# Seven block products for gate and up, and a separate down stage fed through DRAM, in a two-layer hybrid encoder step

## The chip, the core and the metric

The kernel runs on one NeuronCore of a Trainium2 chip. The metric is the device time of one execution in microseconds; lower is better. The core has five engines that run side by side, each through its own list of instructions in a fixed order: TensorE (PE in the tables; its weight loads are PEld), VectorE (DVE), ScalarE (ACT), GpSimd (POOL) and SyncE (SP), which here only starts transfers. An engine that waits for something holds up all that stands behind it in its list.

## What is computed

Two layers of a streaming encoder act on nine tiles of 128 rows (eight of a prompt, and one, number 4 in the kernel's order, with eight decoding streams of 16 rows), each 1024 wide. Each layer has three mixers, an output projection with a layer norm, and a feed-forward block. Only the last is changed:

```python
def conv_ffn(x, conv_prev, w_gate, w_up, conv_w, conv_b, w_down):
    hg = x @ w_gate
    hu = x @ w_up
    ext = jnp.concatenate([conv_prev.astype(hg.dtype), hg], axis=1)
    conv = conv_b + sum(conv_w[j] * ext[:, j:j + t] for j in range(CONV_W))
    return (jax.nn.gelu(conv) * hu) @ w_down, ext[:, t:]

def finish(...):
    x = layer_norm(ALPHA * x + mix @ w_out, ln1_g, ln1_b)
    f, conv_state = conv_ffn(x, conv_prev, w_gate, w_up, conv_w, conv_b, w_down)
    x = layer_norm(ALPHA * x + f, ln2_g, ln2_b)
```

`w_gate` and `w_up` are 1024 x 2816, `w_down` is 2816 x 1024. The 2816 columns are handled as 22 blocks f of 128.

## The kernel before

Every large product is done on float32 numbers that are split in two float32r parts, a high part h (a cast, on ScalarE) and a low part l (the difference, on VectorE or GpSimd). `mm3` (L171) makes one product of three matmuls: h with h, h with l, l with h. Weights come from DRAM as slabs: `load_slab` (L103) fetches a raw half, casts it, subtracts, and puts the parts in one of two buffers; `next_slab` (L141) hands them out in the order of the list `plan`.

After the mixers each layer has these stages. **w_out**: `w_out` adds the output projection to the residual tiles `x1s[j]`, tiles 0 to 4 (`G1`) among the last of the attention, tiles 5 to 8 (`G2`) after it; `norm1` normalises them, and `transpose_into` turns them (TensorE, L201) into `xts[j]`, split by `put_hl` (L191, L192). **Gate and up**: for each f, `gate_up` makes the gate product over three groups of columns (320, 320 and 512 of the 1152 rows), `conv_in` and `conv` apply the convolution and the GELU, then come three up products, `gated` multiplies and splits the result into `ah` and `al`, which stay in SBUF. **Down**: after block 0, and then after every three blocks (`FG`), `down` makes 18 products (nine tiles, two halves of the output) and VectorE adds each to `x1s[j]` (L1322). In the last of these eight passes `norm2` (L224 to L230) normalises each tile when it is done; in layer 0 the tiles are turned for the next layer (`ready`, three tiles behind), in layer 1 they are the output.

Inside one engine the order is set by the program's order and by a scheduler that moves an instruction ahead of others where it is ready earlier. What stands in the list runs in that order.

## Time and profile before

| | us |
|---|---|
| median of three runs (3004.11 to 3006.88) | 3004.44 |
| the profiled execution, its own time | 3001.13 |
| its span, first to last instruction | 2999.4 |
| TensorE busy in the span | 2902.6 (97%) |
| VectorE busy | 1773.2 (59%) |
| ScalarE busy | 1250.6 (42%) |
| GpSimd busy | 612.4 (20%) |

All sums are made against the profiled execution. It lies 3.3 us under the median. A busy TensorE is not yet one at its best: matmuls overlap, so how long one takes is read from the distance between two starts, not from its own duration. Where TensorE is busy without a gap, only fewer or shorter matmuls shorten the stage; where it has gaps, the wait that ends last decides.

### The profile page before, as it was taken

What the parts mean: (1) busy time and instruction counts of PE and PEld (TensorE: products, weight loads), DVE (VectorE), ACT (ScalarE), POOL (GpSimd) and SP (SyncE); (2) the same over time, 40 slices, a digit from 0 to 9 for tenths busy, and PEclk for the clock granted to TensorE, in tenths of its full rate; (3) what the DMA queues carried; (4) which work ended last, traced back from release to release, by engine and by line L of the source; (5) the groups of instructions that cost most, each with busy time, mean ns of one, the idle gap of its engine ahead of it and who ended that gap; (6) DMA issues with size and microseconds to landing.
All of it is one profiled execution on the core that took longest, in us unless ns stands there. A gap on an engine that the chain in (4) does not pass through costs nothing.

```text
span 2999.4 us, 47327 instructions
## 1 busy us (share of the span) xinstructions
PE 2902.6 (97%) x18356; PEld 2642.0 (88%) x18356; DVE 1773.2 (59%) x4110; ACT 1250.6 (42%) x2685; POOL 612.4 (20%) x737
## 2 busy tenths in 40 slices
PE   9999999999999999999999999999999999999997
PEld 8898898998898898898788988989988988988986
DVE  6899777764334334334779996777643333333337
ACT  6588566543222222222356884666331222222212
POOL 3344433420000000000343445334100000000003
PEclk9999999999999999999999999999999999999998
DMA  4211123121111111111222111131211111111112
GB/s 137 62 47 53 41 60 114 45 85 43 50 36 43 50 36 43 50 36 39 100 64 82 44 44 45 47 113 38 92 53 39 36 53 39 36 53 39 36 50 80
DMA packets 79071, 168.92 MB, mean 56 GB/s; under 512 B 18278, under 2 KB 38654, under 8 KB 78846
## 3 DMA queue, kind: packets, MB, share of 16 engines
q1 hardware_dynamic: 71022, 159.99, 16.5%
q10 hardware_dynamic: 7824, 5.90, 0.6%
q8 instruction: 145, 2.38, 0.3%
q14 instruction: 80, 0.66, 0.1%
HBM read 146.60 MB, written 19.25 MB: 55 GB/s over the span
## 4 chain that ended last, share of the span: by engine, by line
PE 84%; DVE 9%; issue 2%; POOL 2%; ACT 2%; DMA 1%; SPq 0%; ACTq 0%; DVEq 0%; POOLq 0%
PE pg L173 12%; PE pg L174 12%; PE pg L175 12%; PE pdn L174 6%; PE pdn L173 6%; PE pdn L175 6%; PE pwo L173 2%; PE pwo L175 2%; PE pwo L174 2%; PE pvg L173 2%; PE pvg L174 2%; PE pvg L175 2%; PE tp L980 1%; DVE spare L555 1%; PE lgi L411 1%
## 5 line engine op out<-in xcount | busy, mean ns | idle before, releaser
L173 PE MATMUL pg<-xg,slab_h 128*128 128x320 f32 (+1 forms) x2112 | 709.0, 336 | 1.1 <-ACT xg L191 1.1
L174 PE MATMUL pg<-xg,slab_h 128*128 128x320 f32 (+1 forms) x2112 | 709.8, 336 | 0.0
L175 PE MATMUL pg<-xg,slab_l 128*128 128x320 f32 (+1 forms) x2112 | 709.1, 336 | 0.0
L173 PEld LDWEIGHTS pg<-xg,slab_h 128*128 128x128 f32 x2112 | 396.4, 188 | 30.2 <-ACT xg L191 1.6
L175 PEld LDWEIGHTS pg<-xg,slab_l 128*128 128x128 f32 x2112 | 396.5, 188 | 28.2
L174 PEld LDWEIGHTS pg<-xg,slab_h 128*128 128x128 f32 x2112 | 396.4, 188 | 27.7
L113 ACT CAST slab_h<-raw 128x1024 fp32r<-128x1024 f32 (+3 forms) x154 | 140.5, 959 | 628.9 <-PE pdn L175 426.1
L1322 DVE SCALAR_TENSOR_TENSOR x<-x,pdn 128x512 f32<-128x512 f32 x288 | 194.5, 684 | 251.0 <-PE pdn L175 249.1
L173 PE MATMUL pdn<-slab_h,ah 128*128 128x512 f32 x792 | 312.5, 395 | 0.0
L174 PE MATMUL pdn<-slab_l,ah 128*128 128x512 f32 x792 | 312.2, 395 | 0.0
L175 PE MATMUL pdn<-slab_h,al 128*128 128x512 f32 x792 | 312.1, 394 | 0.0
L561 ACT ACTIVATE spare<-sc,cand 128x384 bf16<-128x384 f32 (+4 forms) x262 | 244.5, 933 | 67.6 <-DVE cand L587 27.9
L1256 DVE SCALAR_TENSOR_TENSOR ct<-hx,cwt,ct 128x1024 f32<-128x1024 f32 x88 | 113.1, 1285 | 229.9 <-ACT ct L1252 228.3
L1259 POOL COPY tails<-hx 128x16 f32<-128x16 f32 x44 | 9.4, 214 | 1121.5 <-ACT hx L1249 1121.5
L1268 DVE TENSOR_TENSOR ct<-ct,pg 128x320 f32<-128x320 f32 x132 | 72.8, 554 | 233.6 <-PE pg L175 174.2
L121 POOL TENSOR_TENSOR slab_l<-raw,slab_h 128x512 fp32r<-128x512 f32 (+1 forms) x140 | 188.5, 1374 | 102.2 <-ACT slab_h L120 99.9
L175 PEld LDWEIGHTS pdn<-slab_h,al 128*128 128x128 f32 x792 | 149.2, 188 | 34.9
L174 PEld LDWEIGHTS pdn<-slab_l,ah 128*128 128x128 f32 x792 | 149.2, 188 | 34.5
L173 PEld LDWEIGHTS pdn<-slab_h,ah 128*128 128x128 f32 x792 | 149.2, 188 | 34.5
L114 DVE TENSOR_TENSOR slab_l<-raw,slab_h 128x1024 fp32r<-128x1024 f32 (+3 forms) x154 | 166.3, 1112 | 15.7 <-ACT slab_h L113 15.6
L173 PE MATMUL pwo<-slab_h,xg 128*128 128x256 f32 x576 | 165.3, 287 | 0.3
L175 PE MATMUL pwo<-slab_h,xg 128*128 128x256 f32 x576 | 162.9, 283 | 0.6 <-DVE xg L997 0.6
(323 smaller groups left out, 6713.2 us busy)
## 6 DMA issues: line engine op xcount, KB each, us to landing
raw<-w_gu SPq DMA_DIRECT2D x88, 512.0 KB, 4.2
raw<-w_d SPq DMA_DIRECT2D x56, 384.0 KB, 3.6
raw<-w_s SPq DMA_DIRECT2D x40, 512.0 KB, 4.2
raw<-w_o SPq DMA_DIRECT2D x32, 512.0 KB, 4.5
ml<-mixd SPq DMA_DIRECT2D x18, 320.0 KB, 3.0
x<-x SPq DMA_DIRECT2D x9, 512.0 KB, 6.2
xd<-x SPq DMA_DIRECT2D x9, 512.0 KB, 3.0
x<-xd SPq DMA_DIRECT2D x9, 512.0 KB, 7.5
```

The source lines that it names most:

```text
L113: nc.scalar.copy(h[:, s], raw)
L114: eng.tensor_tensor(l[:, s], raw, h[:, s].bitcast(F32), ALU.subtract)
L121: eng.tensor_tensor(l[:, t], raw[:, r], h[:, t].bitcast(F32), ALU.subtract)
L173: nc.tensor.matmul(out, lh, rh, start=first, stop=False)
L174: nc.tensor.matmul(out, lh, rl, start=False, stop=False)
L175: nc.tensor.matmul(out, ll, rh, start=False, stop=last)
L411: nc.tensor.matmul(lg[:, :wh], qTs[j][:, h, :], kflat[:, s], start=True, stop=True)
L555: nc.vector.tensor_scalar(junkv[:, :w], sc[i], cand[q][:, c:c + 1].bitcast(F32), float(kof(i) - w), op0=ALU.is_lt, op1=ALU.add, accum_out= ...
L561: nc.scalar.activation(junka[:, :w], sc[i], AF.Sign, bias=cand[q][:, c:c + 1].bitcast(F32), scale=-1.0, accum_out=dst)
L1256: nc.vector.scalar_tensor_tensor(cpr, hp[s_], cwt[:, f, s_:s_ + 1], cpr, op0=ALU.mult, op1=ALU.add)
L1268: nc.vector.tensor_tensor(ct[:, cs], ct[:, cs], pg[1, c][:, :w], ALU.mult)
L1322: nc.vector.scalar_tensor_tensor(x1s[j][:, cs], x1s[j][:, cs], ALPHA if g == 0 else 1.0, po, op0=ALU.mult, op1=ALU.add)
```

## The change

For each f the matrix of weights is seen as two by two blocks: gate and up, times the two halves of the 1024 inputs (A11, A12 for gate, A21, A22 for up). The inputs are seen as two by two blocks too: the halves of the 1024 inputs, times two sets of rows (prompt tiles 0 to 3 with half of the decoding rows, 5 to 8 with the other half). The four results, which took eight block products, are made of seven, by Winograd's form of Strassen's method:

- Four combinations of the weights, S1 to S4, are made for each f by GpSimd (`wnext`: four instructions of 128x512), then split like any weight.
- Four combinations of the inputs, T1 to T4, are made once for each layer, in `pair` for tiles 5 to 8 and in `pair_dec` for the decoding rows, on GpSimd, VectorE and ScalarE. All operands stay in SBUF: `ar` holds B11, B21, T3 and T4, `ara` B22, `arb` T1, `art` T2.
- A product (`product`) has 24 matmuls for each of two groups of 288 columns over half of the inputs: 12 of each. Its result lies in two PSUM banks. Four such pairs of banks are there.
- VectorE adds the seven results up (`add`, `gate_in`), then come convolution, GELU and multiplication as before.
- The gated rows of each f are written to DRAM (`ad`) in float32, not split. The down stage comes after all 22 blocks: six passes (`FD`: 2, then five times 4 blocks), for which `load_a` and `load_w` fetch and split rows and weights again. The sums are held in new tiles `acc[j]`: ScalarE copies the first pass, VectorE adds the others, and the residual, which was saved to DRAM (`x1d`), is added in passes 2 and 3.
- Weights everywhere go through one tile `ring`, whose parts are laid out by hand. The tiles of the next layer (`xts`) share `ar` with the gated rows of the last pass, so that tiles 4 to 8 are turned only after its last matmul; before, this was so for fewer of them.

```diff
-FG = [(0, 1)] + [(f, 3) for f in range(1, 22, 3)]
+FD = [(0, 2), (2, 4), (6, 4), (10, 4), (14, 4), (18, 4)]
...
+        def pair(j, where):
+
+            va, vb = turned_x(x1s[j], where)
+            at = cols_of(j - 5)
+            t1, t2, t3 = (temp().rearrange("p (k t) -> p k t", k=4) for _ in range(3))
+            nc.scalar.copy(t3, va)
+            sub2(at, t1, "B11", t3, (G, G))
+            put(at, "B22", vb, V)
+            V.tensor_tensor(t2, vb, t1, ALU.subtract)
+            V.tensor_tensor(t3, vb, t3, ALU.subtract)
+            put(at, "T1", t1, V)
+            put(at, "T2", t2, V)
+            rsub2(at, t2, "B21", t2, (G, G))
+            put(at, "T3", t3, V)
+            put(at, "T4", t2, V)
...
         def norm1(j):
             if j in G2:
                 norm_rows(x1s[j], xp1)
             affine_rows(x1s[j], gt, bt, NORM1[j])
+            nc.scalar.dma_start(x1d[j], x1s[j])
...
+            if n == "S2":
+                G.tensor_tensor(tail[:, 0:512], a21, a22, ALU.add)
+                G.tensor_tensor(a21, a11, a21, ALU.subtract)
+                G.tensor_tensor(a11, tail[:, 0:512], a11, ALU.subtract)
+            if n == "S4":
+                G.tensor_tensor(a12, a12, a11, ALU.subtract)
+            h, l = wslot((4 + i) % 8)
+            nc.scalar.copy(h, src)
+            V.tensor_tensor(l, src, h.bitcast(F32), ALU.subtract)
...
+        def product(n, f, x):
+
+            h, l = aw.pop((n, f))
+            xo, b = opx[x], banks("pg")
+            for c in range(2):
+                cs = slice(288 * c, 288 * c + 288)
+                for k in range(4):
+                    mm3(b[:, c, :288], h[:, k, :], l[:, k, :], xo[:, 0, k, cs], xo[:, 1, k, cs], k == 0, k == 3)
...
+        first = [product("A11", 0, "B11")]
+        pair(5, where())
+        pair(6, where())
+        first.append(product("A12", 0, "B21"))
+        pair(7, where())
+        pair(8, where())
+        pair_dec()
...
-            for k in range(KC):
-                    mm3(b[:, :w], hv[:, a, k, :], lv[:, a, k, :], xg[:, 0, k, x0:x0 + w], xg[:, 1, k, x0:x0 + w],
-                        k == 0, k == KC - 1)
...
+        for f in range(NF):
+            b1, b2 = first if f == 0 else (product("A11", f, "B11"), product("A12", f, "B21"))
...
+            nc.scalar.copy(s1, b1[:, :, :288])
+            gate_in(f, 0, s1, b2)
+            add(s1, s1, product("S2", f, "T2"))
...
+            add(s2, s1, product("S1", f, "T1"))
+            gate_in(f, 1, s2, product("S4", f, "B22"))
+            conv(f)
+            b7 = product("S3", f, "T3")
+            add(s2, s2, b7)
+            add(s3, s1, b7)
+            gated(f, 1, s2)
+            add(s3, s3, product("A22", f, "T4"))
+            gated(f, 0, s3)
+            nc.scalar.dma_start(ad[f], ct[f % 2])
...
+                if g == 0:
+                    nc.scalar.copy(acc[j][:, cs], po)
+                else:
+                    V.tensor_tensor(acc[j][:, cs], acc[j][:, cs], po, ALU.add)
+                if u % 4 == 0 and nxt:
+                    f = nxt.pop(0)
+                    load_a(f)
+                    load_w(g + 1, f)
```

Three places of the order matter. The first is TensorE's list where gate and up begin, before: `pg` is a product of gate and up, `trx` the turning of a tile, and tiles 5 to 8 (`x1_5` to `x1_8`) are turned after four products of block 0.

```order
L175 MATMUL pg_8996<-xg1_79,slab_l_8736 128x320
L201 MATMUL trx_9021<-identr_72,x1_5_8297 128x128 x4
L201 MATMUL trx_9028<-identr_72,x1_5_8297 128x128 x4
L201 MATMUL trx_9035<-identr_72,x1_6_8299 128x128 x4
L201 MATMUL trx_9042<-identr_72,x1_6_8299 128x128 x4
L201 MATMUL trx_9049<-identr_72,x1_7_8301 128x128 x4
L201 MATMUL trx_9056<-identr_72,x1_7_8301 128x128 x4
L201 MATMUL trx_9063<-identr_72,x1_8_8303 128x128 x4
L201 MATMUL trx_9070<-identr_72,x1_8_8303 128x128 x4
L173 MATMUL pg_9084<-xg2_80,slab_h_8735 128x512
```

The same place of TensorE's list in the changed kernel, where the second product (`pg_8984`, A12 with B21) ends: `art` is T2 and `arb` is T1.

```order
L178 MATMUL pg_8984<-ar_75,ring_76 128x288
L1238 MATMUL trx_9009<-identr_66,x1_7_8280 128x128 x8
L1238 MATMUL trx_9035<-identr_66,x1_8_8282 128x128 x8
L176 MATMUL pg_9113<-art_8891,ring_76 128x288
L176 MATMUL pg_9141<-arb_8269,ring_76 128x288
```

Two products stand ahead of the last turning instead of four, and the matmul behind it reads T2, which needs all four tiles and the decoding rows. GpSimd's list at that place, in the changed kernel, for tiles 7 and 8 and the beginning of the decoding rows (`x12d`); `tail` is the temporary for T1, `temp0` that for T2 and T4, `temp1` that for T3:

```order
L1261 TENSOR_TENSOR tail_77<-temp1_8274,ar_75 128x512
L1267 TENSOR_TENSOR temp0_8273<-temp0_8273,ar_75 128x512
L1262 TENSOR_TENSOR tail_77<-tail_77,ar_75 128x512
L1266 TENSOR_TENSOR temp0_8273<-ar_75,temp0_8273 128x512
L1261 TENSOR_TENSOR tail_77<-temp1_8274,ar_75 128x512
L1267 TENSOR_TENSOR temp0_8273<-temp0_8273,ar_75 128x512
L1262 TENSOR_TENSOR tail_77<-tail_77,ar_75 128x512
L1261 TENSOR_TENSOR tail_77<-x12d_8275,ar_75 128x256
L1266 TENSOR_TENSOR temp0_8273<-ar_75,temp0_8273 128x512
```

GpSimd had only a few copies of at most 16 columns at this place before; now four instructions of 128x512 stand there for each of four tiles and twelve of half that size for the decoding rows, and every tile uses the same three temporaries. VectorE's list there, in the changed kernel, for one tile (6; the first row and the last two are its neighbours'):

```order
L1229 TENSOR_TENSOR ar_75<-temp0_8273,ar_75 128x4x128
L1279 TENSOR_TENSOR temp0_8273<-trx_8958,tail_77 128x512
L1280 TENSOR_TENSOR temp1_8274<-trx_8958,temp1_8274 128x512
L1229 TENSOR_TENSOR arb_8269<-tail_77,arb_8269 128x4x128
L1229 TENSOR_TENSOR art_8891<-temp0_8273,art_8891 128x4x128
L1229 TENSOR_TENSOR ar_75<-temp1_8274,ar_75 128x4x128
L1229 TENSOR_TENSOR ara_8268<-trx_9009,ara_8268 128x4x128
L1229 TENSOR_TENSOR ar_75<-temp0_8273,ar_75 128x4x128
```

T2's temporary is written only after the low part of the former tile's T4 (the first row), and GpSimd's second pair of instructions waits for the low part of T2 (the fifth).

## Rows read from the trace of the kernel before

**Rows 1.** Page, part 1: busy time, share of span, instructions of each engine
```profile
PE 2902.6 (97%) x18356; PEld 2642.0 (88%) x18356; DVE 1773.2 (59%) x4110; ACT 1250.6 (42%) x2685; POOL 612.4 (20%) x737
```

**Rows 2.** Windows: from:to, length, busy by engine (instructions), granted clock, DMA share, GB/s
```profile
654.60:1484.30 829.70, 828.12 (x4401) 733.98 (x4400) 344.78 (x495) 211.04 (x341) 29.67 (x99) 1.00 0.14 45
...
2148.20:2980.50 832.30, 831.61 (x4403) 736.39 (x4401) 349.11 (x499) 209.03 (x336) 32.95 (x101) 1.00 0.14 44
2980.50:2999.40 18.90, 0.00 (x0) 0.00 (x0) 15.08 (x18) 2.48 (x2) 9.86 (x6) 0.59 0.35 139
```

**Rows 3.** Timeline, TensorE, gate and up: start, duration (us), engine, line, operation
```profile
999.74 0.31 PE L174 MATMUL pg<-xg,slab_h 128*128 128x320 f32 x1
...
1003.85 0.31 PE L175 MATMUL pg<-xg,slab_l 128*128 128x320 f32 x1
...
1005.38 0.39 PE L173 MATMUL pg<-xg,slab_h 128*128 128x512 f32 x1
...
1009.23 0.39 PE L175 MATMUL pg<-xg,slab_l 128*128 128x512 f32 x1
```

**Rows 4.** Timeline, TensorE, w_out: products of 256 columns
```profile
634.97 0.28 PE L173 MATMUL pwo<-slab_h,xg 128*128 128x256 f32 x1
...
639.88 0.28 PE L175 MATMUL pwo<-slab_h,xg 128*128 128x256 f32 x1
```

**Rows 5.** Timeline, TensorE, where tiles 5 to 8 are turned in layer 0
```profile
668.85 3.66 PE L201 MATMUL trx<-identr,x 128*128 128x128 f32 x32
673.06 0.88 PE L173 MATMUL pg<-xg,slab_h 128*128 128x512 f32 x3 [0.56 <-ACT xg L191]
```

**Rows 6.** Timeline, VectorE, end of norm1 of tiles 7 and 8 in layer 0
```profile
664.72 2.35 DVE L230 TENSOR_TENSOR x<-x,ct 128x1024 f32<-128x1024 f32 x2
```

**Rows 7.** Groups by form, GpSimd: count, busy us, mean ns, idle before
```profile
L121 POOL TENSOR_TENSOR slab_l<-raw,slab_h 128x512 fp32r<-128x512 f32 x136 | 182.8, 1371 | 102.0 <-ACT slab_h L120 99.8 <-PE lg L949 2.0
...
L366 POOL TENSOR_TENSOR vbuf<-vbuf,both 128x256 f32<-128x256 f32 x2 | 1.5, 732 | 0.0
```

**Rows 8.** Groups by form, VectorE
```profile
L1256 DVE SCALAR_TENSOR_TENSOR ct<-hx,cwt,ct 128x1024 f32<-128x1024 f32 x88 | 113.1, 1285 | 229.9 <-ACT ct L1252 228.3
...
L1257 DVE SCALAR_TENSOR_TENSOR ct<-hx,cwt,ct 128x128 f32<-128x128 f32 x88 | 31.0, 352 | 192.0 <-ACT ct L1252 190.5
L1268 DVE TENSOR_TENSOR ct<-ct,pg 128x512 f32<-128x512 f32 x44 | 30.2, 687 | 166.1 <-PE pg L175 166.1
L1270 DVE TENSOR_TENSOR al<-ct,ah 128x512 fp32r<-128x512 f32 x44 | 30.1, 685 | 0.0
```

**Rows 9.** Groups by form, ScalarE
```profile
L191 ACT CAST xg<-trx 128x512 fp32r<-128x512 f32 x72 | 39.3, 605 | 27.2 <-PE trx L201 27.2
```

**Rows 10.** Timeline, VectorE, end of layer 1
```profile
2976.27 1.21 DVE L229 TENSOR_TENSOR x<-x,hx 128x1024 f32<-128x1024 f32 x1
...
2979.45 1.66 DVE L229 TENSOR_TENSOR x<-x,hx 128x1024 f32<-128x1024 f32 x1
...
2985.13 0.68 DVE L1322 SCALAR_TENSOR_TENSOR x<-x,pdn 128x512 f32<-128x512 f32 x1
```

**Rows 11.** Timeline, GpSimd, the same place
```profile
2977.62 2.41 POOL L230 TENSOR_TENSOR x<-x,ct 128x1024 f32<-128x1024 f32 x1 [1.24 <-DVE bnsc L224]
```

**Rows 12.** Windows of 4 us where layer 1 begins, columns as in rows 2
```profile
1492.00:1496.00 4.00, 0.00 (x0) 0.00 (x0) 4.00 (x7) 0.00 (x0) 4.00 (x3) 0.97 0.55 162
1496.00:1500.00 4.00, 3.27 (x15) 3.27 (x16) 3.50 (x6) 3.27 (x5) 2.63 (x3) 0.50 0.61 231
1500.00:1504.00 4.00, 4.00 (x23) 4.00 (x23) 3.82 (x4) 2.24 (x4) 4.00 (x3) 0.68 0.43 151
```

**Rows 13.** Waits of TensorE, 1465 to 1545 us: us in total, times, longest
```profile
PE trx L201 <- POOL x L230: 6.3, 2, 5.3
PE kt L170 <- DVE ks L340: 3.9, 1, 3.9
```

**Rows 14.** Page, part 6: transfers, count, KB each, median us to landing
```profile
raw<-w_gu SPq DMA_DIRECT2D x88, 512.0 KB, 4.2
```

More of the change, by code (lines that the diff above doesn't have):

```diff
@@ L105, in load_slab @@
         n = src.shape[-1]
-        h = slabp.tile([P, 2368], F32R, tag="sh", name="slab_h")[:, :n]
-        l = slabp.tile([P, 2368], F32R, tag="sl", name="slab_l")[:, :n]
+        i = load_slab.i
+        load_slab.i += 1
+        m = i % 19
+        o = 0 if m % 2 == 0 else 4736 if m == 1 else 4096
+        h, l = ring[:, o:o + n], ring[:, o + n:o + 2 * n]
         for c in range(2):
@@ L122, in load_slab @@
         return h, l
+    load_slab.i = 0
     plan = []
@@ new lines, in put, with turned_x @@
+        def put(at, n, src, eng):
+            nc.scalar.copy(at(n, 0), src)
+            eng.tensor_tensor(at(n, 1), src, at(n, 0).bitcast(F32), ALU.subtract)
+        def turned_x(src, where):
+            out = []
+            for c in range(2):
+                b = where(c)
+                bv = b.rearrange("p (k t) -> p k t", k=4)
+                for k in range(4):
+                    nc.tensor.transpose(bv[:, k, :], src[:, (4 * c + k) * P:(4 * c + k + 1) * P], ident)
+                out.append(bv)
+            return out
@@ L1191, in norm1, with pair_dec @@
+        def pair_dec():
+            at = cols_of(4)
+            t1, t2, t3 = (temp()[:, :256].rearrange("p (k c t) -> p k c t", k=4, c=2) for _ in range(3))
+            sub2(at, t1, "B11", x12d, (G, G))
+            put(at, "T1", t1, G)
+            rsub2(at, t2, "B22", t1, (G, G))
+            put(at, "T2", t2, G)
+            rsub2(at, t3, "B22", x12d, (G, G))
+            put(at, "T3", t3, G)
+            rsub2(at, t2, "B21", t2, (G, G))
+            put(at, "T4", t2, G)
         def norm1(j):
@@ L1199, in hybrid_encoder @@
             slab = next_slab(d["w_o"][L, s])
+            if s == 3:
+                for _ in range(4):
+                    wnext()
             for j in G2:
@@ new lines, in gated, with load_a @@
+        def gated(f, h, b):
+            cp_, cd_ = halves_of(ct[f % 2], h)
+            V.tensor_tensor(cp_, cp_, prompt(b), ALU.mult)
+            V.tensor_tensor(cd_, cd_, rows(b), ALU.mult)
+        wdv = {}
+        avs = {}
+        def load_a(f):
+            o = 2304 * ((f + 2) % 8)
+            ah, al = ar[:, o:o + 1152], ar[:, o + 1152:o + 2304]
+            for c in range(2):
+                s_ = slice(576 * c, 576 * c + 576)
+                rw = asp.tile([P, 576], F32, tag="araw", name="araw")
+                nc.sync.dma_start(rw, ad[f][:, s_])
+                nc.scalar.copy(ah[:, s_], rw)
+                V.tensor_tensor(al[:, s_], rw, ah[:, s_].bitcast(F32), ALU.subtract)
+            avs[f] = (ah, al)
@@ new lines, in load_w @@
+        def load_w(g, f):
+            f0, nf = FD[g]
+            rw = rawp.tile([P, 1184], F32, tag="raw", name="raw")
+            nc.sync.dma_start(rw[:, :D], d["w_d"][L, f])
+            for nh in range(2):
+                q = (4 + 2 * f0 + nh * nf + f - f0) % 16
+                if q < 8:
+                    h, l = wslot(WSLOT[q])
+                else:
+                    t, o = (art, q - 8) if q < 12 else (wdv["x"], q - 12)
+                    h, l = t[:, 1024 * o:1024 * o + 512], t[:, 1024 * o + 512:1024 * o + 1024]
+                cs = slice(512 * nh, 512 * nh + 512)
+                nc.scalar.copy(h, rw[:, cs])
+                V.tensor_tensor(l, rw[:, cs], h.bitcast(F32), ALU.subtract)
+                wdv[f, nh] = (h, l)
@@ new lines, in hybrid_encoder @@
+        gs_.close()
+        as_.close()
+        ops_.close()
+        pst.close()
+        pst = ExitStack()
+        banks_open(pst)
+        st0 = ExitStack()
+        ac2 = pool(f"ac2_{L}", 1, st=st0, right=True)
+        ws_ = ExitStack()
+        ac1 = pool(f"ac1_{L}", 1, st=ws_, right=True)
+        acc = [(ac1 if j in G1 else ac2).tile([P, D], F32, name=f"acc{j}") for j in range(NT)]
+        asp = pool(f"at{L}", 2, st=ws_, right=True)
+        wsp = pool(f"ws{L}", 1, st=ws_, right=True)
@@ L1380, in hybrid_encoder @@
+        ready(DEC)
+        ws_.close()
         fst.close()
```

361 lines of the change are left out of this document (209 added, 152 removed).

## The prediction

> **What bounds the kernel now.** I first read the busy times [rows 1]: TensorE 97%, all others far below. That average hides two kinds of stage, so I cut the span at the ends of w_out and of the down stage [rows 2]. From w_out's end to the end of down, TensorE is busy for 828.1 of 829.7 us in layer 0 and for 831.6 of 832.3 in layer 1, at the full clock (1.00, 2.4 GHz). Nothing but the number and length of matmuls matters there. The last stretch, 18.9 us, has no TensorE work: VectorE finishes the last norms.
>
> What a matmul costs is read from distances between starts. With 320 columns, 28 steps take 1003.85 - 999.74 = 4.11 us, 146.8 ns each; with 512, 17 steps take 3.85 us, 226.5 ns [rows 3]; with 256, 41 steps take 4.91 us, 119.8 ns [rows 4]. A column costs (226.5 - 146.8)/192 = 0.415 ns and a matmul some 13.5 ns on top of that. The new width, 288, lies halfway between 256 and 320: 133.3 ns.
>
> **The change part by part.**
>
> *Seven products.* Before, a block f has 2 x 2 x 8 x 3 = 96 matmuls of 320 columns and 48 of 512: 96 x 0.1468 + 48 x 0.2265 = 24.96 us. After, 7 x 24 = 168 of 288: 22.39 us. Over 44 blocks (two layers) that is 44 x 2.57 = 113 us less, all on the path. An eighth of the columns goes (6912 of 55296), yet time falls by 10.3%, as 24 matmuls more pay their fixed part.
> Weighed against this: the Trainium skill ("TensorE: Matmul & The Clock Gate", on 56 against 53.3 ns) puts the fixed part at about 2.5 ns per matmul; by it the gain would be 44 x (6912 columns at 0.4167 ns - 24 x 2.5 ns), some 124 us, an estimate from that page. The rows give 13.5 ns in this kernel, and the measurement decides.
>
> *Steady pace of the blocks.* TensorE sets it only if the others need less than 22.4 us for a block. VectorE: 11 instructions of 512 columns (seven weight differences, two of gate_in, two of gated) at 0.687, five adds of 576 at about 0.77, two of 1024 at 1.285, six small at up to 0.35 [rows 8]: 7.6 + 3.9 + 2.6 + 2.1 = 16.2 us. GpSimd: 4 x 1.37 = 5.5 us [rows 7]. ScalarE about 9, at 0.605 for 512 columns [rows 9]. Where VectorE must stand still for all of GpSimd's time, it needs 21.7, just under 22.4. Weights are made seven products ahead (21 us); raw weights land in 4.2 us [rows 14]; a PSUM pair is needed again 9.6 us after it was filled. So I cost this at nothing, with TensorE as the cover; the margin, 0.7 us at worst, is thin, and that is a rival below.
>
> *The beginning of the stage.* Before, norm1 of tile 8 ends at 667.1 [rows 6], 12 us after w_out, beneath four products of block 0 (14.1 us); the turning follows, and TensorE waits 0.56 us [rows 5]. After, TensorE has two products (48 x 0.133 = 6.4 us) and the turning (3.7 us), together 10.1 us, and then stands before S2 x T2, which needs T2 for all tiles. That chain I follow from w_out's end. Norms of 7 and 8 and tile 5's operands share VectorE, so the low part of tile 5's T2 ends at about 17 us. From one tile to the next GpSimd does four instructions, at 1.3 us 5.2 us; then VectorE does two subtractions and two differences, 2.6 us with the hand-overs, before GpSimd may go on: 7.8 us. The temporaries are shared, so no tile overlaps the next. Three more tiles: 17 + 3 x 7.8 = 40.4 us. The decoding rows follow: two instructions of 512 and seven of 256 on GpSimd (2.7 + 7 x 0.75 [rows 7]) and a cast (about 0.4): 48.8.
> Such short steps disturb each other: VectorE's 128x1024 product takes 1.21 us alone and 1.66 us when it begins during GpSimd's L230; it then ends at 2981.11, 1.08 us after GpSimd's end at 2980.03 [rows 10, 11]. It was held until GpSimd was done. In one tile's round that hits two differences, about 0.6 us each: 9.0 us instead of 7.8, and with the end about 53 us instead of 49.
> The Trainium skill ("SBUF — State Buffer", Who interferes with whom) says that VectorE instructions with two SBUF inputs and GpSimd instructions that read SBUF shut each other out for a whole instruction, while those that take one input from PSUM do not. The rows agree; by the rule the wait is 43 us, without it 39.
> I take 53 - 10 = 43 us of waiting. Then the clock: where TensorE stood still at 1492 to 1496, it ran at 0.50 for the next 4 us and at 0.68 for another 4 [rows 12], so at 1.2 GHz for about 6.6 us, 3.3 us of work lost. Together 46 us a layer, 92 us. Bounds: 33 a layer if the steps go as fast as their lone times and the first tile starts at once; 56 if GpSimd is slowed to 1.5 us.
>
> *Down.* The products are the same 54 x 22 matmuls of 512 a layer. Loads now come twice, but 1.1 MB for each block in 12.2 us of matmuls; only pass 2 must be filled during the short pass 1 (24.5 us, four blocks, 4.4 MB, so 181 GB/s; the trace shows 231 GB/s in one window [rows 12]), and the list starts these fetches in the last block of gate and up. Pass 1's copies stand in ScalarE's list between casts that wait for fetches; eight PSUM banks cover 10.9 us. I put 2 us a layer here, 4 us in all; 0 to 12 a layer are the bounds.
>
> *Layer boundary.* Before, TensorE waits 6.3 + 3.9 us and some in 1465 to 1545 [rows 13], and runs at half clock twice: VectorE has fallen behind in the last pass, whose tile took 18 x 0.2265 = 4.1 us. Now a tile takes 24 x 0.2265 = 5.4 us, the first weights of layer 1 have a free place early, and tiles 4 to 8 are turned while three products that need only 0 to 2 run (10 us). I expect 10 us less (bounds: 0 and 16).
>
> *The end.* Of 18.9 us, VectorE's backlog is 2985.13 - 2980.5 = 4.6 us and the norm of tile 7 [rows 2, 10]. At 5.4 us a tile it keeps up: 8 us less (4 to 10).
>
> *The rest* (the stores of `x1d` and `ad`, the ring) has no waiter: the order of the attention stages hardly moves. 0, within 6 us either way.
>
> Sum: 3001.1 - 113 + 92 + 4 - 10 - 8 = 2966; the median lies 3.3 above the profiled execution, so 2969 us.
>
> **The rivals.**
>
> 1. *The beginning is hidden after all.* If tiles overlap and the wait is 12 us a layer: 2969 - 2 x 34 = 2901. For it: the work is small (60 us of three engines' time). Against: one set of temporaries, and TensorE's list has nothing else to do.
> 2. *Fetches hold up down.* 12 us a layer rather than 2: 2989. For: every row goes through DRAM twice, in half-size buffers of which there are two. Against: 4.2 us to landing and early fetches.
> 3. *VectorE sets the pace of gate and up: slower.* Its place is the list from S4's sum to the last gating, where casts, GpSimd and VectorE wait for each other in turn. If a block takes 24.5 us: + 44 x 2.1 = 92, 3061. It is slower than before from 22.4 + 35/44 = 23.2 us a block. For: 21.7 at worst, before any wait in the list. Against: 16.2 of work, and slack of 9.6 us in PSUM.
> 4. *The products don't get shorter.* If a 288-column matmul took 146.8 ns as with 320 (a floor by the weight load), a block would take 24.7 us: 3070. Against: 256 columns run at 119.8.
>
> **How the numbers follow.** The forecast, with its bounds (2930 to 2995), 0.64; rival 1 0.08; rival 2 0.10; rival 3 0.11; rival 4 0.02; another that I don't see 0.05. The range 2928 to 3003 takes in the forecast and rival 2, and cuts off 1, 3 and 4. About 0.2% (6 us) is what a measurement of this kernel can tell from no change. Faster by more than that: 0.64 + 0.08 + 0.10, and 0.03 of the rest, 0.85; within it 0.04; slower 0.11.
>
> **What would show it.** Each block at 22.4 us between its first products, with starts 133 ns apart, shows the gain. A wait of S2's first product near 43 us, once a layer, ended by ScalarE's cast or GpSimd's difference of T2, shows the beginning; a round of 8 to 9 us from one tile's T2 to the next shows its cause. No gap over 3 us at down's first passes, TensorE's waits at the boundary under 4 us, and some 11 us from the last matmul to the end show the rest. The forecast is wrong if blocks take over 23 us, if T2's wait is under 25 or over 60 us, or if the attention stages change length by more than 6 us.

## The result and the profile after

The changed kernel takes 2967.24 us (median of four runs, 2962.09 to 2973.71) against 3004.48 in the same measurement: a ratio of 0.9875, with a 95% interval of 0.9852 to 0.9899. The forecast was 2969. The profiled execution took 2963.75 us, its span is 2961.9; against the span of before that is 37.5 us less.

Busy times of the page, to be read against [rows 1]:

```profile
PE 2791.9 (94%) x19412; PEld 2616.6 (88%) x19412; DVE 2072.2 (70%) x4706; ACT 1375.6 (46%) x2881; POOL 937.4 (32%) x927
```

TensorE is busy 110.7 us less, yet the span shrinks by 37.5: the rest are new gaps. The windows by stage say where (from:to, length, busy by engine, granted clock, DMA share, GB/s). They are gate and up in layer 0; in it the blocks 1 to 21 alone; down in layer 0; gate and up, then down, in layer 1; the end:

```profile
657.60:1196.10 538.50, 499.32 (x3729) 498.00 (x3728) 352.68 (x571) 203.91 (x323) 173.91 (x181) 0.96 0.22 77
727.50:1196.10 468.60, 468.60 (x3530) 468.39 (x3528) 308.81 (x508) 177.58 (x279) 134.97 (x143) 1.00 0.23 81
1196.10:1483.30 287.20, 281.05 (x1227) 228.69 (x1227) 157.01 (x241) 73.82 (x122) 30.78 (x21) 0.99 0.35 118
...
2131.70:2670.50 538.80, 499.37 (x3729) 497.93 (x3727) 351.67 (x569) 203.88 (x323) 173.73 (x181) 0.96 0.22 77
2670.50:2951.40 280.90, 276.17 (x1193) 224.38 (x1192) 151.76 (x233) 65.91 (x107) 21.06 (x15) 0.99 0.33 107
2951.40:2961.90 10.50, 0.00 (x0) 0.00 (x0) 7.42 (x9) 0.73 (x1) 3.29 (x2) 0.60 0.35 134
```

From the second row, 21 blocks take 468.6 us, 22.31 each, with TensorE busy all the time. Before, three blocks took 75.02 us, from the first product (`pg`) to the first of down (`pdn`) behind them, 25.01 each:

```profile
721.64 0.31 PE L173 MATMUL pg<-xg,slab_h 128*128 128x320 f32 x1
...
796.66 0.40 PE L173 MATMUL pdn<-slab_h,ah 128*128 128x512 f32 x1
```

So 44 blocks are worth 118 us. The first block is the other side of it: the distance from its first product to that of block 1 is 68.7 us in layer 0 and 70.3 in layer 1, 46.4 and 48.0 over a regular block.

Where these go is seen in TensorE's timeline at the start of the stage in layer 0 (start, duration, engine, line, operation, in brackets the idle time before it and who ended it); `trx` is the turning, `art` is T2:

```profile
658.85 0.37 PE L176 MATMUL pg<-ar,ring 128*128 128x288 f32 x1 [1.14 <-DVE x L1160]
...
662.11 1.95 PE L1238 MATMUL trx<-identr,x 128*128 128x128 f32 x16
...
671.97 1.94 PE L1238 MATMUL trx<-identr,x 128*128 128x128 f32 x8 [4.74 <-ACT art L1228]
681.63 1.94 PE L1238 MATMUL trx<-identr,x 128*128 128x128 f32 x8 [7.72 <-ACT art L1228]
709.15 0.61 PE L176 MATMUL pg<-art,ring 128*128 128x288 f32 x1 [25.57 <-ACT art L1228]
```

4.7 + 7.7 + 25.6 = 38.0 us of waiting. The first two are tiles 7 and 8, which wait for a pair of PSUM banks (four pairs; two hold the first products, two the tiles before them): the profile names a cast, but VectorE's last reading of tile 5's pair, L1280, ends at the same moment, 671.8. Behind them is the same chain, and the last wait ends with it. GpSimd, and then VectorE, for one round of that chain (`ara` is B22):

```profile
682.77 1.64 POOL L1266 TENSOR_TENSOR temp<-ar,temp 128x512 f32<-128x512 f32 x1 [3.22 <-DVE art L1229]
684.37 1.26 POOL L1261 TENSOR_TENSOR tail<-temp,ar 128x512 f32<-128x512 f32 x1
685.60 1.26 POOL L1267 TENSOR_TENSOR temp<-temp,ar 128x512 f32<-128x512 f32 x1
686.82 1.26 POOL L1262 TENSOR_TENSOR tail<-tail,ar 128x512 f32<-128x512 f32 x1
691.29 1.65 POOL L1266 TENSOR_TENSOR temp<-ar,temp 128x512 f32<-128x512 f32 x1 [3.22 <-DVE art L1229]
```

```profile
684.48 0.69 DVE L1229 TENSOR_TENSOR ara<-trx,ara 128x512 fp32r<-128x512 f32 x1 [1.20 <-ACT ara L1228]
687.54 1.08 DVE L1229 TENSOR_TENSOR ar<-temp,ar 128x512 fp32r<-128x512 f32 x1 [2.37 <-ACT ar L1228]
688.73 0.69 DVE L1279 TENSOR_TENSOR temp<-trx,tail 128x512 f32<-128x512 f32 x1
689.34 0.68 DVE L1280 TENSOR_TENSOR temp<-trx,temp 128x512 f32<-128x512 f32 x1
689.94 0.68 DVE L1229 TENSOR_TENSOR arb<-tail,arb 128x512 fp32r<-128x512 f32 x1
690.53 0.68 DVE L1229 TENSOR_TENSOR art<-temp,art 128x512 fp32r<-128x512 f32 x1
```

A round, 691.29 - 682.77, is 8.52 us: GpSimd works for 5.3 and then stands for 3.2, until VectorE's four short steps (688.73 to 691.21) are done. VectorE's second row shows the holding: the low part of T4, which begins during GpSimd's last instruction (to 688.08), takes 1.08 us where others take 0.68.

### The profile page after: what moved, and what is told of

The parts are those of the page before. It is cut to its first block, busy times and chain, and to the rows that moved or that the text cites. A ratio compares the mean times of both kernels' runs of the same rounds, so it can differ in the third digit from the quotient of the medians.

```text
span 2961.9 us, 51451 instructions
## 1 busy us (share of the span) xinstructions
PE 2791.9 (94%) x19412; PEld 2616.6 (88%) x19412; DVE 2072.2 (70%) x4706; ACT 1375.6 (46%) x2881; POOL 937.4 (32%) x927
## 4 chain that ended last, share of the span: by engine, by line
PE 77%; DVE 11%; DMA 3%; issue 3%; POOL 3%; ACT 2%; SPq 0%; ACTq 0%; DVEq 0%; POOLq 0%
PE pg L178 11%; PE pg L176 11%; PE pg L177 11%; PE pdn L176 6%; PE pdn L178 6%; PE pdn L177 6%; PE pwo L176 2%; PE pwo L178 2%; PE pwo L177 2%; PE pvg L176 2%; PE pvg L177 2%; PE pvg L178 2%; PE tp L989 1%; DVE spare L562 1%; DMA raw<-w_d 1%
## 5 line engine op out<-in xcount | busy, mean ns | idle before, releaser
L176 PE MATMUL pg<-ar,ring 128*128 128x288 f32 x1408 | 414.6, 294 | 1.1 <-DVE x L1160 1.1
L178 PE MATMUL pg<-ar,ring 128*128 128x288 f32 x1408 | 415.3, 295 | 0.0
L177 PE MATMUL pg<-ar,ring 128*128 128x288 f32 x1408 | 414.5, 294 | 0.0
L1341 ACT CAST ring<-raw 128x512 fp32r<-128x512 f32 x264 | 163.6, 620 | 454.8 <-PE pg L177 417.9
L128 POOL TENSOR_TENSOR ring<-raw,ring 128x512 fp32r<-128x512 f32 (+1 forms) x140 | 193.7, 1409 | 323.2 <-ACT ring L127 275.6
L1342 DVE TENSOR_TENSOR ring<-raw,ring 128x512 fp32r<-128x512 f32 x264 | 204.5, 775 | 110.5 <-ACT ring L1341 106.9
L568 ACT ACTIVATE spare<-sc,cand 128x384 bf16<-128x384 f32 (+4 forms) x262 | 244.3, 932 | 74.7 <-DVE cand L594 30.4
L176 PEld LDWEIGHTS pg<-ar,ring 128*128 128x128 f32 x1408 | 264.1, 188 | 1.3 <-issue 1.3
L178 PEld LDWEIGHTS pg<-ar,ring 128*128 128x128 f32 x1408 | 264.1, 188 | 0.0
L177 PEld LDWEIGHTS pg<-ar,ring 128*128 128x128 f32 x1408 | 264.1, 188 | 0.0
L1597 DVE TENSOR_TENSOR acc<-acc,pdn 128x512 f32<-128x512 f32 x180 | 122.8, 684 | 179.3 <-PE pdn L178 178.0
L1493 DVE TENSOR_TENSOR s<-s,pg 128x576 f32<-128x576 f32 x220 | 164.2, 748 | 53.6 <-PE pg L178 50.9
L176 PE MATMUL pwo<-ring,ar 128*128 128x256 f32 x576 | 167.1, 290 | 0.0
L178 PE MATMUL pwo<-ring,ar 128*128 128x256 f32 x576 | 164.0, 285 | 0.0
L177 PE MATMUL pwo<-ring,ar 128*128 128x256 f32 x576 | 164.0, 285 | 0.0
L562 DVE TENSOR_SCALAR_CACHE_REDUCE spare<-sc,cand 128x384 bf16<-128x384 f32 (+3 forms) x208 | 158.2, 761 | 1.4
L176 PE MATMUL pdn<-ring,ar 128*128 128x512 f32 x360 | 140.9, 391 | 2.9 <-DVE s L1493 2.9
L178 PE MATMUL pdn<-ring,ar 128*128 128x512 f32 x360 | 140.8, 391 | 0.0
L177 PE MATMUL pdn<-ring,ar 128*128 128x512 f32 x360 | 140.7, 391 | 0.0
```

The costliest lines, as they stand in the source:

```text
L128: eng.tensor_tensor(l[:, t], raw[:, r], h[:, t].bitcast(F32), ALU.subtract)
L176: nc.tensor.matmul(out, lh, rh, start=first, stop=False)
L177: nc.tensor.matmul(out, lh, rl, start=False, stop=False)
L178: nc.tensor.matmul(out, ll, rh, start=False, stop=last)
L562: nc.vector.tensor_scalar(junkv[:, :w], sc[i], cand[q][:, c:c + 1].bitcast(F32), float(kof(i) - w), op0=ALU.is_lt, op1=ALU.add, accum_out= ...
L568: nc.scalar.activation(junka[:, :w], sc[i], AF.Sign, bias=cand[q][:, c:c + 1].bitcast(F32), scale=-1.0, accum_out=dst)
```

## Experiments

Each kernel is the changed one with the edit shown, timed beside the kernel before; times are medians, "first block" is the distance named above in layers 0 and 1. Its median of 2967 is the yardstick. Runs of one kernel lie up to 12 us apart, so differences of a few us are read from the stage, not from the time.

**no_operands: what the whole beginning costs.** Reads B11 and B21 in place of all other operands and leaves out their making, with the turning of tiles 5 to 8.

```diff
-            xo, b = opx[x], banks("pg")
+            xo, b = opx["B21" if x in ("B21", "T2", "T3") else "B11"], banks("pg")
...
-        pair(5, where())
-        pair(6, where())
...
-        pair(7, where())
-        pair(8, where())
-        pair_dec()
```

> Left out: the turning of tiles 5 to 8 and the whole of pair and pair_dec; products that read T1 to T4 or B22 read B11 or B21 instead, so gate and up are not what the reference computes. Everything else, the norms and the weight sums among it, stays. It prices the beginning of the stage. Chain theory: the first block of a layer takes 68.7 and 70.3 us where all others take 22.3; all of the excess, 46.3 and 48.0 us, comes from preparing the operands, so the time falls from 2967 to about 2873 (between 2868 and 2880), and the first block takes 22.3 to 24 us. Rival: part of the excess is the backlog of VectorE's norms and of the weight sums, which would hold the first products just as long; then the first block still takes 30 to 40 us and the time is 2890 to 2915.

2883.51 us, ratio 0.959 (0.9576 to 0.9604): 84 us less, between the two expectations. The first block takes 28.3 and 30.4 us. Preparing the operands is 80 of the 94 us by which the two first blocks exceed regular ones; some 6 to 8 us a layer remain, of which TensorE waits 10.7, in the two layers together, for ScalarE's first copy out of PSUM:

```profile
PE pg L176 <- ACT s L1498: 10.7, 2, 6.6
```

**dec_first: the decoding rows out of the chain's end.**

```diff
         opx["T2"] = operand(art, 0)
+        pair_dec()
...
-        pair_dec()
```

> pair_dec is called before the tiles 5 to 8, whose data it does not need, right after the last of w_out; same arithmetic. Chain theory: everything before S2 x T2 is one chain, and the decoding rows are its last link, from T2's low part of tile 8 at 699.7 to the end of T2's decoding rows at 710.6 in layer 0. GpSimd is idle for most of 650 to 665, so its 12 short instructions (8.6 us) cost nothing there: 9 to 10 us less a layer, the time is about 2948. Rival: GpSimd's work among the last norms holds VectorE's two-input instructions (as at the end of before, 1.66 us for 1.21) and the chain begins later by as much as it is shorter: 2960 to 2967.

2951.98 us, 0.9815 (0.9801 to 0.983); first block 61.0 and 63.6, so 7.7 and 6.7 less instead of 9 to 10. In layer 0 a part of it has only moved: the first product waits 4.6 us for VectorE's last sum of w_out (L1160), 1.1 in the changed kernel, so that from w_out's end to block 1 only 4.3 us are gained there, and 6.7 in layer 1. Both views were partly right: the link is gone, but GpSimd's work for the decoding rows now falls among the norms, and VectorE's norm steps wait for it. Here the last of these instructions (GpSimd), and a step of 1.2 us that takes 1.7 beside it (VectorE):

```profile
662.86 1.28 POOL L1229 TENSOR_TENSOR ar<-temp,ar 128x256 fp32r<-128x256 f32 x1 [0.52 <-ACT ar L1228]
```

```profile
663.48 1.74 DVE L234 TENSOR_TENSOR x<-x,ct 128x1024 f32<-128x1024 f32 x1
...
682.05 0.68 DVE L1229 TENSOR_TENSOR art<-temp,art 128x512 fp32r<-128x512 f32 x1
```

The low part of T2 of tile 5 (VectorE's second row) begins 20.2 us after w_out's end at 661.8; in the changed kernel 15.9.

**dec_early: the same, earlier.** `pair_dec` in the third of w_out's four slabs. T3 and T4 of the decoding rows are then written to parts of `ar` that w_out still reads, so w_out works on other data.

```diff
+                if s == 2 and j == 6:
+                    xg1s.close()
...
+                    pair_dec()
...
-        pair_dec()
```

> Only pair_dec is moved, to where two more thirds of w_out's products for tiles 5 to 8 are still to come (the third of four slabs), so that GpSimd's short instructions no longer fall among the last norms. In dec_first the first block took 61.0 and 63.6 us, 7.7 and 6.7 less than in the changed kernel, and T2 of tile 5 came 4.3 us later after w_out than there. If it was GpSimd among the norms that took those 4 us, they come back: 57 and 59 us, and the time is some 7 us under dec_first's, 2945. If T2 of tile 5 is late for another reason (the order that VectorE's list got), it stays at 2950 to 2955.

2960.42 us, 0.9855 (0.9838 to 0.9871); first block 58.4 and 60.1, close to what was expected of GpSimd being out of the norms' way. The time is not: w_out waits for those casts, 8.7 us in each layer, and without them it would be some 2943.

```profile
PE pwo L176 <- ACT ar L1228: 8.7, 1, 8.7
```

**own_temps: tiles that may overlap.**

```diff
-            t1, t2, t3 = (temp().rearrange("p (k t) -> p k t", k=4) for _ in range(3))
+            own = x1s[j][:, 0:512], x1s[j][:, 512:1024], temps[1 + j % 2]
+            t1, t2, t3 = (t.rearrange("p (k t) -> p k t", k=4) for t in own)
```

> Each of the tiles 5 to 8 gets temporaries of its own: T1's and T2's stand in the tile itself, which nobody reads once it is turned and stored, T3's alternate between two. Same arithmetic. Shared-temporaries theory: a round of 8.52 us is four GpSimd instructions (5.3) and then, with GpSimd idle for 3.2 us, four of VectorE; with temporaries of their own the tiles overlap, GpSimd is the bound, and a round takes 5 to 6 us: 3 rounds give 7.5 to 10 us a layer, the time is about 2949. Exclusion theory: VectorE's low parts read two SBUF operands and wait for a GpSimd instruction to end (as T4's low part does, 1.09 us for 0.68), so four GpSimd instructions and four such low parts still follow each other, 5.0 + 4 x 0.65 = 7.6 us a round: 2 to 3 us a layer, the time is about 2962.

2943.06 us, 0.9788 (0.9773 to 0.9802). First block 62.2 and 64.5, 6.5 and 5.8 less: between the two theories. T2's low parts of tiles 5 to 8, from VectorE's timeline:

```profile
677.87 0.68 DVE L1229 TENSOR_TENSOR art<-x,art 128x512 fp32r<-128x512 f32 x1
...
679.07 1.75 DVE L1229 TENSOR_TENSOR art<-x,art 128x512 fp32r<-128x512 f32 x1
...
692.57 0.68 DVE L1229 TENSOR_TENSOR art<-x,art 128x512 fp32r<-128x512 f32 x1
...
695.44 0.68 DVE L1229 TENSOR_TENSOR art<-x,art 128x512 fp32r<-128x512 f32 x1
```

Tiles now come in pairs, 14.7 us from one pair to the next (677.87 to 692.57), 7.35 a tile: overlap ends at two. Tiles 7 and 8 need the PSUM banks of 5 and 6, but tile 7 is turned by 676.5; what it waits for then is its T3 temporary, of which there are two, so that 7 shares one with 5. ScalarE's copy into it is released by the low part of tile 5's T3:

```profile
679.24 0.59 ACT L1277 COPY temp<-trx 128x512 f32<-128x512 f32 x1 [1.24 <-DVE ar L1229]
```

In GpSimd's list, T4's first steps of tiles 5 and 6 (678.63 and 680.96) stand ahead of tile 7 as well. Where VectorE and GpSimd meet, low parts take 1.75 us instead of 0.68. The time fell by twice as much as the first blocks: 10 us come from down (280.9 and 277.3 us), where the edit touches nothing but ScalarE's list came out with one copy ahead of a cast; copy_v, below, tests what that is worth.

**pair_v: one engine instead of two.**

```diff
-            sub2(at, t1, "B11", t3, (G, G))
+            sub2(at, t1, "B11", t3, (V, V))
...
-            rsub2(at, t2, "B21", t2, (G, G))
+            rsub2(at, t2, "B21", t2, (V, V))
```

> In pair the four subtractions and additions of each tile that GpSimd made (those with B11 and B21) are made by VectorE; the decoding rows stay with GpSimd, and the three temporaries stay shared. VectorE has 11 instructions a tile, which start 0.60 us apart where nothing holds them: 6.6 us, against a round of 8.52. Hand-over theory: what costs is that GpSimd takes 1.25 us for what takes VectorE 0.6, and that the two wait in turn; a round falls to 6.6 to 7.2, 4 to 6 us less a layer, the time is about 2957. Rival: VectorE still has the norms of tiles 7 and 8 to make when the chain begins (to 673), so the first tile's operands come later by what is moved onto it, and the rounds, in order on one engine, wait for ScalarE's casts: 2963 to 2972, no gain.

2949.83 us, 0.9812 (0.9792 to 0.9833); first block 61.9 and 63.4, so 6.8 and 6.9 less, where 4 to 6 were expected. The round is 6.86 us, eleven VectorE instructions 0.60 to 0.71 us apart, where the hand-over theory put it, with the temporaries still shared. The same step of tiles 6 to 8:

```profile
680.29 0.69 DVE L1279 TENSOR_TENSOR temp<-trx,tail 128x512 f32<-128x512 f32 x1
...
687.15 0.69 DVE L1279 TENSOR_TENSOR temp<-trx,tail 128x512 f32<-128x512 f32 x1
...
694.01 0.69 DVE L1279 TENSOR_TENSOR temp<-trx,tail 128x512 f32<-128x512 f32 x1
```

**sums_more: how thin is the cover in the blocks?**

```diff
-                G.tensor_tensor(tail[:, 0:512], a21, a22, ALU.add)
+                for _ in range(5):
+                    G.tensor_tensor(tail[:, 0:512], a21, a22, ALU.add)
```

> The first of the four weight sums of each block is written five times over, the same values each time: GpSimd has eight instructions of 128x512 in a block in place of four, some 10 us instead of 5.1. It asks how thin the cover is under which VectorE's work in a block lies. If VectorE stands still for GpSimd's whole time in two-input instructions, it needs 16.2 + 10 = 26 us a block at worst, and blocks grow from 22.31 to somewhere between 24 and 26 us: 74 to 160 us more, 3040 to 3130. If only the instructions that happen to meet are held, and the list has slack, the blocks stay at 22.3 us and the time at 2962 to 2975.

2971.02 us, 0.9882 (0.9867 to 0.9896): no difference that counts, and blocks of 22.31 us as before. Seventeen blocks of the changed kernel, and of this one (columns as above):

```profile
794.40:1173.70 379.30, 379.30 (x2859) 379.30 (x2858) 248.81 (x409) 140.18 (x221) 113.66 (x120) 1.00 0.22 75
```

```profile
800.20:1179.40 379.20, 379.20 (x2858) 379.20 (x2858) 251.78 (x408) 134.92 (x219) 201.79 (x186) 1.00 0.22 74
```

GpSimd goes from 6.7 to 11.9 us a block; VectorE's busy time, in which being held counts, from 14.6 to 14.8. The full price, VectorE standing still for all of GpSimd's time, isn't paid. At the beginning of the stage the extra sums do show: from w_out's end to block 1 72.5 and 73.4 us pass, against 69.8 and 70.2.

**copy_v: down's first pass.**

```diff
-                    nc.scalar.copy(acc[j][:, cs], po)
+                    V.tensor_copy(acc[j][:, cs], po)
```

> In the down stage's first pass the results are copied out of PSUM by VectorE instead of ScalarE. In the changed kernel the second pass waits 4.1 and 2.7 us for such a copy (and layer 0 runs at half clock for 4 us after it); ScalarE's list has the copies behind casts that wait 2.5 us for the fetch of w_d. List theory: VectorE's list is free of those waits, so the copies come in time: the gap falls under 1 us, some 3 to 6 us a layer, the time is 2957 to 2962. Rival: VectorE's low parts wait for the same casts, so its list stands just as long: no change, 2964 to 2970.

2958.89 us, 0.9843 (0.9827 to 0.9859). In the changed kernel the second pass begins in layer 0 with the first row below (TensorE), which waits for a copy in ScalarE's list; that copy, the last row of the second fence, stands behind a cast that waits for w_d:

```profile
1228.03 0.79 PE L176 MATMUL pdn<-art,ar 128*128 128x512 f32 x1 [4.09 <-ACT acc L1595]
```

```profile
1226.08 0.62 ACT L1488 CAST ring<-raw 128x512 fp32r<-128x512 f32 x1 [2.48 <-DMA raw<-w_d]
1226.82 0.67 ACT L1472 CAST ar<-araw 128x576 fp32r<-128x576 f32 x1
1227.39 0.58 ACT L1595 COPY acc<-pdn 128x512 f32<-128x512 f32 x1
```

With the copies on VectorE the same matmul waits 0.4 us:

```profile
1224.87 0.47 PE L176 MATMUL pdn<-art,ar 128*128 128x512 f32 x1 [0.40 <-DVE acc L1595]
```

Down gets shorter by 3.3 and 0.6 us, less than the 3 to 6 a layer that were expected: in layer 0 two waits of 1.2 and 0.9 us for copies remain just ahead of this matmul, and the granted clock is still 0.60 in 1226 to 1230. The profiled spans lie 10.4 us apart; 5.0 of that is in the layer boundary and the attention of layer 1 (643.4 for 648.4), which the edit doesn't touch, and isn't its doing as far as the runs show. That the time came out in the expected range is partly luck.

**Can the chain be shortened further?** Five kernels tried. t2_first_v gives each tile storage of its own, makes both steps of T1 on VectorE and, in the program's order, T2 ahead of T1's parts, T3 and T4 (only tile 5's T1 and T3 come before tile 8), and takes dec_early's place for `pair_dec`, with the same overwriting of w_out's data:

```diff
+            sub2(at, t1, "B11", t3, (V, V))
+            V.tensor_tensor(t2, vb, t1, ALU.subtract)
+            put(at, "T2", t2, V)
...
+        for r in rests + lasts:    # T1, T3; then T4
+            r()
```

> Same arithmetic, other order: each tile has its own T1 and T2 temporaries (in the tile itself), only what T2 needs and what frees PSUM comes first for all tiles (copy, the two subtractions with B11, on VectorE, then T2, T3's difference and B22), then the parts of T1 and T3, last T4 (its two steps with B21 on GpSimd); pair_dec is called while w_out still runs. Chain theory: T2 of all tiles needs 7 VectorE instructions a tile, 0.60 us apart, 4.2 us; from T2 of tile 5 at about 16 us after w_out three more tiles give 29, minus 10 us of TensorE's work: a wait of 15 to 20 us a layer in place of 38, and the decoding rows' 10 us are gone too. First block some 46 to 52 us in place of 68.7 and 70.3; the time is about 2920 (2910 to 2930). Rival: once T2 is early, T1, T3 and T4 are late, because the same instructions stand behind it; the first block stays over 58 us, and the time is that of own_temps, 2943, or more.

2947.32 us, 0.9804 (0.979 to 0.9819); first block 54.7 and 54.0, of which the forecast was 46 to 52, and again 8.7 us a layer of w_out's wait. VectorE is busy almost without a gap up to S2's start, the norms of tiles 7 and 8 among it.

best_v and best_g put the parts together, with w_out's data left alone; best_g has one of the two steps of T1 on GpSimd:

```diff
+            sub2(at, t1, "B11", va, (V, V))    # best_g: (V, G)
+            V.tensor_tensor(t2, vb, t1, ALU.subtract)
+            put(at, "T2", t2, V)
+            put(at, "B22", vb, V)
...
+        # later: T1's parts; T3 = T2 - B11 (G, G); T4 (V, V)
```

> Same values, the parts put together: T1 is formed straight from PSUM (no copy ahead of it) and T3 later as T2 - B11, each tile works in its own storage, T2 comes first and T3 and T4 last for all tiles; T1 and T2 of the decoding rows are made while w_out still runs, but T3 and T4, whose places w_out still reads, after it; all four tiles are turned after the first product, so that the last no longer waits for PSUM behind the second; four weight splits that nobody needs yet come after T2; down's first pass is copied by VectorE. Chain theory: T2 of a tile costs VectorE four instructions of 0.60 us and B22 one more, 3.0 us; with the last norms, about 8 us after w_out, T2 of tile 8 ends some 22 us after w_out's end, of which TensorE has 10 to do: waits of 10 to 15 us a layer, first block 40 to 46 us instead of 68.7 and 70.3, and the time is 2895 to 2915. Rival: T1, T3 and T4 are late instead, at the fourth to seventh product: first block over 52 us, 2930 or more.

> As best_v, with the second step of T1 (minus the low part of B11) on GpSimd: VectorE has four instructions a tile in the chain instead of five, 2.4 us, but each tile's T1 takes 1.25 us and two hand-overs on GpSimd, and where GpSimd reads SBUF, VectorE's low parts are held (1.75 us for 0.68 in own_temps). If VectorE's sum is what counts, it is 2 us a layer faster than best_v; if hand-overs and exclusion count, 3 to 6 us a layer slower: 6 to 12 us above best_v.

2950.98 us (0.9822, 0.9808 to 0.9837) and 2953.10 (0.9831, 0.9814 to 0.9847), first blocks 57.8 and 63.3, and 59.3 and 61.9: the expectation of 2895 to 2915 was wrong, the rival's numbers came out, but not its reason: in layer 0 of best_v TensorE waits 14.6 us at the turnings and 8.5 in S2, and nowhere behind it. The two kernels can't be told apart. In best_v VectorE is busy for 42.1 of the 45.5 us between w_out's end and T2 of tile 8:

```profile
661.70:707.20 45.50, 18.27 (x94) 16.89 (x93) 42.12 (x58) 15.67 (x25) 21.39 (x16) 0.72 0.23 75
```

In the changed kernel it is 32.6 of 51.5. So all of T2 was there 6 us earlier (in the changed kernel the decoding rows come last, at the end of that stretch), but the free time was used up: the scheduler filled VectorE with whatever was ready. t2_ahead forces the order:

```diff
+        with tc.issue_after(ends[0].ins), tc.issue_after(ends[1].ins):
+            # T1's parts, T3, T4 and the weight splits, behind T2 of tile 8
```

> As best_v, but the order is now forced: T1's parts, T3, T4 and the six weight splits that are not needed yet stand behind T2 of tile 8 on ScalarE and VectorE, T4's steps with B21 go to GpSimd, T3's to VectorE. In best_v VectorE was busy without a gap up to T2 of tile 8 at 707, 45 us after w_out, and of that time more than a third went to instructions that T2 doesn't need (T1's, T3's and T4's parts, weight splits) or to waiting for GpSimd's sums of the next block. VectorE-order theory: with these behind it, 8 us of norms and 20 instructions of 0.60 us bring T2 of tile 8 to some 21 to 24 us after w_out: first block 38 to 46 us instead of 57.8 and 63.4, and the time is 2900 to 2920. Rival: what was put behind is then late for S1, S3 and A22, product by product, and the first block stays above 52 us: 2940 or more; then the stage is bound by the sum of VectorE's work (some 45 us a layer) and no order of it helps.

2948.10 us, 0.9795 (0.9776 to 0.9815). S2 is no longer waited for: its products run from 688.6. But the wait moved: the third product of the rest, S4 with B22, needs a PSUM pair, which ScalarE's copy frees, and in ScalarE's list that copy stands behind the casts of T4 and a split that waits for GpSimd. TensorE waits 19.9 us a layer there, and the first block takes 59.9 and 63.9; it is the rival's size, in one wait at S4 instead of product by product:

```profile
PE pg L176 <- ACT s L1518: 39.8, 2, 19.9
```

own_early is own_temps and copy_v with `pair_dec` early, but the casts of T3 and T4 after w_out, and with the weight sums of block 1 behind the last step of T4:

```diff
+                    pair_dec()    # in the third slab; sums, T1 and T2
...
+        later.pop()()             # after w_out: the parts of T3 and T4
```

> own_temps with one thing more at the beginning of the stage, and the copies of copy_v: all sums of the decoding rows, and their T1 and T2, are made while w_out still runs (only the casts and low parts of their T3 and T4, whose places w_out reads, come after it), and the weight sums of block 1 are queued behind the last step of T4, where own_temps had them. In own_temps T2 of tile 8 was done at 696.1 and T2 of the decoding rows at 706.4, so these rows held S2 x T2 for the last 9 us. If they do it because they stand at the chain's end, that time comes off: first block 53 to 56 us instead of 62.2 and 64.5, some 17 us in all, and 3 to 6 us more in down: about 2922. Rival, as best_v and t2_ahead came out: what is taken away at the front of VectorE's list comes back behind it, as waits for T3, T4 or PSUM: first block 59 us or more, 2938 to 2945.

2940.20 us, 0.9783 (0.9768 to 0.9797). The first block is what was expected in layer 0, 55.5 (58.4 in layer 1), and gate and up take 528.3 and 528.5 us instead of 538.4 and 538.8. The time isn't the 2922 that follows: in the profiled execution w_out of layer 0 ends 8.4 us later (666.1 for 657.7) though TensorE's list up to there is the same. Its largest piece is one wait of 3.1 us at 470 us, 0.65 in the changed kernel, after which the granted clock is 0.50 in 476 to 480. What makes VectorE late there stays open. Together with own_temps it is the fastest of all, 27 us under the changed kernel.

## Why the prediction held

| step | predicted | measured |
|---|---|---|
| 44 blocks | -113 | -118 (25.01 to 22.31 each) |
| beginning of the stage, both layers | +92 | +86 (46.4 + 48.0, less 4.2 a layer of before [rows 5]) |
| down | +4 | +9 |
| layer boundary and attention of layer 1 | -10 | -10 (658.1 to 648.5) |
| end | -8 | -8.5 (18.9 [rows 2] to 10.5) |
| attention of layer 0 | 0 | +3 |

The measured steps add up to -38, against 37.5 between the spans. They miss the prediction by -5, -6, +5 and +3, which nearly cancel: that the total lies within 2 us of the forecast is partly luck. Nor is the agreement at the boundary as close as it looks: in no_operands, own_temps, pair_v and copy_v, which change nothing there, this stretch takes 642.9 to 647.2 us, and w_out of layer 0 ends between 656.6 and 662.9. Down's time before is what is left of the stage, w_out's end to the last product (836.5 us in layer 0, up to 1491.4, 7 us beyond the window in [rows 2]; 831.0 in layer 1), without 22 blocks and the 4.2 us of turning: 282.2 and 276.7, against 287.2 and 280.9.

- **Seven products** was right in its step, too small by 5 us: the starts lie 132.8 ns apart for 133.3, and before, a block took 25.01 for 24.96. By the Trainium skill's fixed part ("TensorE: Matmul & The Clock Gate", on 56 against 53.3 ns) the estimate was 124; the measured 118 lies between it and the rows.
- **The steady pace** was right. VectorE is busy 14.6 us of 22.31, not 16.2, and sums_more shows that the margin isn't thin: rival 3 is refuted even with twice GpSimd's time for the sums.
- **The beginning** was right in mechanism and nearly in size. Predicted: T2 of tile 5 at 17 us after w_out, rounds of 9.0, decoding rows 8.4, end at 53. Measured: low part done at 16.6, rounds of 8.52, 9.4 for the decoding rows, S2 at 51.6. What the sum of waits left out is that 12.5 of the 38.0 us stand at the turnings, for want of PSUM; the wait before S2 alone is 25.6, only just above the 25 below which the prediction called itself wrong. The clock cost more than the 3.3 put down. After the last wait it is 0.50 (1.2 GHz) in the first 4 us and 0.83 in the next, in the rows below, and the five products there take 18.4 us instead of 15.9, so 2.5. After each of the two waits at the turnings, eight matmuls take 1.94 us, where sixteen took 1.95 at 662.11; the granted clock in 671.9 to 674.0 is 0.50. That is another 1.7, together 4.2, and with the 38.0 of waiting close to the 42.2 us that layer 0 lost. Experiments: no_operands prices it as a whole, dec_first, own_temps and pair_v each take 6 to 8 us a layer off by another link of the same chain. Rival 1 needed tiles that overlap; own_temps shows that even then 25 us of wait remain.

```profile
709.00:713.00 4.00, 3.85 (x16) 3.86 (x17) 0.00 (x0) 0.09 (x1) 4.00 (x5) 0.50 0.02 4
713.00:717.00 4.00, 4.00 (x27) 4.00 (x27) 1.91 (x2) 2.19 (x4) 3.96 (x5) 0.83 0.00 0
```

- **Exclusion** was right as a term, but too large: put at 1.2 us a round, it takes 0.4 on VectorE (T4's low part, 1.08 us) and 0.4 on GpSimd (its first instruction takes 1.64 us for 1.26, begun while VectorE makes T3's low part); the other low parts fall where GpSimd stands still. The Trainium skill ("SBUF — State Buffer", Who interferes with whom) fits the rows: what is held has two SBUF inputs, while B22's low part, which reads one input from PSUM, takes 0.69 us at 684.48 with GpSimd at work. It matters more where tiles overlap (1.75 us in own_temps).
- **Down** is the step that was mis-sized. "Eight PSUM banks cover 10.9 us" didn't hold: in layer 0 pass 2 waits 4.1 us for a copy, then runs at a granted clock of 0.50 for its first 4 us (the row below), in layer 1 it waits 2.7; no gap over 3 us had been announced. The cause is the one that the prediction named as a risk: copy_v takes the 4.1 us away, though it wins only 3.9 us in the two layers. In own_temps, whose list came out otherwise, pass 2 waits 0.9 and 1.3 us, the clock after it stays at 1.00, and the whole 9 us are gone (280.9 and 277.3 us, before 282.2 and 276.7). Rival 2, 12 us a layer, was too large.

```profile
1228.00:1232.00 4.00, 3.97 (x9) 3.14 (x10) 2.02 (x4) 3.03 (x6) 0.00 (x0) 0.50 0.52 146
```

- **Boundary and end** were right: TensorE waits 1.9 us in 1483 to 1560, against the waits in [rows 13], and 10.5 us pass from the last product to the end, against some 11 announced.

```profile
PE tb L173 <- DVE qs L383: 1.9, 1, 1.9
```

The expectations of the last five experiments were the wrong ones, in the time above all. Most of them took the chain to T2 as the bound and reckoned its length with VectorE free for it. VectorE wasn't: with the norms, the parts of five operands and the weight splits it is busy, the holding included, for some 45 us between w_out's end and the last operand (23.2 + 22.6 us in t2_ahead's two stretches up to 712), and what t2_ahead puts behind T2 is waited for at S4. What paid was to take work out of the stretch (the decoding rows), to let it overlap, or to move it off the slower engine (pair_v); reordering on top of that won little: t2_first_v, which has the early decoding rows, the move and tiles with storage of their own as well, takes 54.7 and 54.0 us for its first blocks, where dec_early alone takes 58.4 and 60.1.

## What to carry to other kernels

A saving in the number of products is as good as its rows say, but operands made from the last results of the stage before stand on the critical path as a whole: count every engine's instructions there in list order, and look for one shared temporary or PSUM pair that forces them in turn. Before reordering such a stretch, add up the busiest engine's work in it; if it fills the stretch, expect more of less work or an earlier start than of another order. Copies that free PSUM shouldn't stand in a list behind casts that wait for DMA.
